# Where the last two tiles of an input projection stand: beside the delta rule's recurrence, or behind it

## The chip, the core and the metric

The kernel runs on one core of a Trainium2 chip. The metric is the device time of one launch in microseconds, the median of several runs, lower is better. The engines are TensorE (PE in the profile; PEld is its weight load), VectorE (DVE), ScalarE (ACT), GpSimd (POOL) and SyncE (SP), which here only issues transfers. Each engine runs its own list of instructions in order.

## The reference, cut to what matters

Two layers of a transformer are applied to 512 latent tokens and 128 context tokens. Four token mixers stand side by side in a layer. They share one input projection `h @ w_in` and one output projection; a SwiGLU follows. The part that matters is the third mixer, a gated delta rule, whose state `s` is carried from one chunk of 64 tokens to the next:

```python
def mix_latent(h, ...):
    (a_q, a_k, a_v, b_q, b_k, b_v, c_qkv, c_g, c_a, c_b, d_cq, d_ckv, d_kr) = project_in(h, p)
    o_a = gqa_attend(...)                 # grouped-query attention
    o_b = natten_latent(b_q, b_k, ...)    # neighbourhood attention
    o_c, _ = deltanet_mixer(c_qkv, ...)   # forward and backward in time
    o_d = block_attention(...)            # latent attention (MLA)
    return concatenate([o_a, o_b, o_c, o_d]) @ p['w_out']

def step(s, xs):                          # the recurrence of deltanet_mixer
    v_new = u_i - einsum('bhcd,bhde->bhce', w_i, s)
    o_i = einsum('bhcd,bhde->bhce', qd_i, s) + einsum('bhij,bhje->bhie', qk_i, v_new)
    s = s * gl_i[..., None, None] + einsum('bhcd,bhce->bhde', kd_i, v_new)
    return s, o_i
```

After the recurrence the result is normalised per head and gated (`rms_norm(o) * silu(z_g)`).

## The kernel before

Activations are kept feature by feature (128 features on the partitions, 640 tokens along the row). Each float32 operand is split into a high and a low part, so a product of a 128-wide tile of the projection with 1024 input features takes 8 blocks x 3 products x 2 halves of the tokens = 48 matmuls; they are the rows `acc<-h,whi` and `acc<-h,wlo`. A tile's weights come by a transfer into `wst` and are split by ScalarE (`whi`) and VectorE (`wlo`).

TensorE's order is written out at build time. Each piece of work is a Python generator that yields what it waits for (an event, a number of free buffers, a moment); `_Order` keeps a clock of its own with estimated costs, and lets the ready generator of the best rank record its next instructions. The order of the other engines is then fixed by the scheduler of the framework. On the chip each engine runs through its list and waits only for data and buffers. So a `yield` in this code is a wait of the recording, not an instruction.

The work around the change, the same in both layers:

- `delta_chain` makes the operands of the delta rule and then calls `scan` over 8 chunks. A step of `scan` is on TensorE `ks`, `qs`, `ysp`, `spp`, `opp`, eight 64x64 matmuls each (16 records in the trace, as float32 is run in two passes), and between them a VectorE sum `xt` (after `ks`), a ScalarE copy `ysb` (after `ysp`) and a VectorE sum `st`, the new state (after `spp`), on which the next `ks` waits.
- `delta_out` then normalises on VectorE (`dno`, `oss`, a reciprocal root of 11 small instructions, `dno`), transposes on TensorE (`otp`) and gates on VectorE (`og`). It is called for chunks 2 to 5 while the last steps of the scan run, and for the rest behind them.
- `rest` records what is left of the input projection: the parts of the grouped-query attention, two gate tiles, one block of the neighbourhood attention's values (`tm_chunk`), and at last four tiles (`wfm` 8 to 11) that go out to memory through `natst` and `dnat` and are read again much later (`nraw`). It has rank 2, so it fills in between the steps of the scan.
- `attention` begins behind the chain: it casts `og` into `oh`, and starts grouped-query attention (`gqa`, two groups of 8 units). A unit is `sc` (4 matmuls; scores), a maximum on VectorE (`sm`), an exponential on ScalarE (`p`), six transposes (`ptp`), copies (`pt`), and for each two units a product with the values (`pvo`, 14). The second group's keys and queries are transposed on TensorE (`gktp`, `gqtp`) and split by ScalarE and VectorE (`gk`, `qst`). When `rest` has ended, buffers are turned over to a second score bank (`psE`) and to the operands of the latent attention (`mkr`, `mcf`, `mcq`, `wkvup`).

Of the kernel before, what the change touches and what calls it, by code (L numbers as in the profile page):

```python
# [288 lines left out]
class _Build:  # L289
# [622 lines left out]
    def delta_chain(self, l, h, S, dn, dt, ps, pd, first):  # L912

        nc, A, od = self.nc, self.A, self.od
        hr = lambda q, k: h[:, q, k]

        qk = S["qk"] = dn.tile([128, 2, 10, 128], F32, name="qk")
        vn = S["vn"] = dn.tile([128, 10, 2, 64], F32, name="vn")
        kt = S["kt"] = dn.tile([128, 10, 2, 64], F32, name="kt")
        S["ss"] = [dt.tile([128, 10, 2], F32, name=f"ss{i}") for i in range(2)]  # L920
        self.M = dn.tile([128, 2, 10, 2, 64], F32, name="dM")
        self.Q = dn.tile([128, 2, 10, 2, 64], F32, name="dQ")

        def features(fts):
            evs = []
            for ft in fts:
                o = yield from self.fm_steps(A["wfm"][l, ft], hr, range(KD), ps)
                evs.append(od.spawn(self.conv_steps(l, ft, o, S, dt, pd), 0))
            return evs

        ev_k = [od.spawn(self.conv_steps(l, ft, o, S, dt, pd), 0) for ft, o in zip((2, 3), first)]

        g0 = dt.tile([128, 5, 16], F32, name="g0")
        lss = S["lss"] = dt.tile([128, 5, 2], F32, name="lss")

        def sink(t, o):
            st = self.cv.tile([128, 648], F32, tag="cv", name="crow", bufs=4)
            nc.scalar.copy(st[:, 0:432], o)
            nc.vector.tensor_copy(g0[:, t], st[:, 416:432])
            nc.sync.dma_start(out=self.dscr["craw"][l, :, t, :], in_=st[:, 0:416])  # L940
            for i, (a, b) in enumerate(((0, 256), (256, 384))):
                j = dt.tile([128, 512], F32, tag="mst", name="msq", bufs=1)
                nc.scalar.activation(j[:, 0:b - a], st[:, a:b], AF.Square, accum_out=lss[:, t, i:i + 1])

        yield od.spawn(self.tm_chunk([A["wtmc"][l, i] for i in range(4)], h, 432, [(ps, "w")] * 5, sink, "cv"), 0, True)
        S["input"].at = od.now
        gz = dt.tile([128, 10, 2, 2, 2], F32, name="gz")
        gv = g0.rearrange("p t (r a) -> p t r a", r=2)
        for r in range(2):
            for cc in range(2):  # L950
                nc.vector.tensor_copy(gz[64 * r:64 * r + 64].rearrange("p (t c) a d q -> p t c (a d q)", c=2)[:, :, cc, :],
                                      gv[64 * cc:64 * cc + 64, :, r, :])
        ev_g = od.spawn(self.gates(l, gz, dn, dt, pd), 0)

        def more(fts, when):
            for e in when:
                yield e
            ev = yield from features(fts)
            for e in ev:
                yield e  # L960

        for e in ev_k + [ev_g]:
            yield e
        self.key_norms(S["ss"][1], dn, dt)
        yield od.via(("ACT", 0.3), ("DVE", 0.4), ("ACT", 0.2))
        evs = [od.spawn(self.chunk_matrices(g, qk, ev_k, dt, pd), 0) for g in range(5)]
        ev_q = od.spawn(more((0, 1), evs[:1]), 0.8, True)
        ev_v = od.spawn(more((4, 5), [S["inv"]]), 0.9, True)
        ev_m = od.spawn(self.query_matrices(qk, evs + [ev_q], pd), 0.7)
        for e in evs:  # L970
            yield e
        S["inv"].at = od.now
        rt = yield from self.inverse16(l, dt)
        yield od.spawn(self.inverse(rt, dt, pd), 0)
        for e in (ev_v, ev_m):
            yield e
        self.query_norms(S["ss"][0], dn, dt)
        nc.vector.tensor_tensor(out=vn, in0=vn, in1=self.nk.unsqueeze(3).to_broadcast([128, 10, 2, 64]), op=ALU.mult)
        S["O"] = dn.tile([128, 10, 2, 64], F32, name="dno")
        s0 = dn.tile([128, 2, 2, 64], F32, tag="st", name="st", bufs=4)  # L980
        nc.sync.dma_start(out=s0, in_=A["st0"][l])

        def prompt():
            sf = yield from self.scan(range(8, 10), None, S, dn, pd)
            nc.sync.dma_start(out=A["ost"][l], in_=sf)
            yield S["gates"]
            yield from self.delta_out(l, [(8, 10)], S, dn, pd)

        def middle():
            yield S["gates"]  # L990
            yield from self.delta_out(l, [(2, 6)], S, dn, pd)

        yield od.via(("DVE", 1.3))
        e = od.spawn(prompt(), 0.5)
        s6 = yield from self.scan(range(6), s0, S, dn, pd)
        em = od.spawn(middle(), 0.5)
        yield from self.scan(range(6, 8), s6, S, dn, pd, range(8))
        yield S["gates"]
        yield from self.delta_out(l, [(0, 2), (6, 8)], S, dn, pd)
        yield e  # L1000
        yield em
# [985 lines left out]
    def mixer(self, l, h, h_st, x, fx, fx_st, P, W, p_side, w_side):  # L1987
# [10 lines left out]
            first = self.start(h, x, fx, ps)  # L1998
        od = self.od = _Order(w=1 if l == 0 else 5, dn=3, ta=3, cv=4, **{t: 0 for t in "sc fd pv wt p pt k0 q0 k1 q1".split()})
        S = {"heads": [], "group": [_Event(), _Event()]}  # L2000
        S.update({k: _Event() for k in ("inv", "gates", "h", "input", "back", "whole")})
        ready = []

        def second_half():
# [27 lines left out]
        def rest():  # L2032
            for c in range(2):
                yield from self.tm_chunk([A["wtma"][l, c, i] for i in range(2)], h, 256, [(ps, "w")] * 3,
                                         lambda t, o, c=c: nc.scalar.copy(ar[:, t, 256 * c:256 * c + 256], o))
            norms.append(od.spawn(self.gqa_norm(l, ar, dn, dt, S["inv"]), -0.5))
            heads.append(od.spawn(ahead(), 0.3))
            for i in range(2):
                o = yield from self.fm_steps(A["wfm"][l, 6 + i], hr, range(KD), ps)
                for hf in range(2):  # L2040
                    nc.scalar.activation(og[:, i, SPLIT[hf]], o[hf], AF.Silu)
                od.give("w", 2, od.via(("ACT", 0.8)))
            S["gates"].at = od.now + 1.0

            def sink_v(t, o):
                st = self.cv.tile([128, 648], F32, tag="cv", name="bvst", bufs=4)
                nc.scalar.copy(st[:, 0:256], o)
                nc.sync.dma_start(out=self.dscr["bv"][l, 128 * t:128 * t + 128], in_=st[:, 0:256])

            yield from self.tm_chunk([A["wtma"][l, 2, i] for i in range(2)], h, 256, [(ps, "w")] * 3, sink_v, "cv")  # L2050
            for i in range(4):
                o = yield from self.fm_steps(A["wfm"][l, 8 + i], hr, range(KD), ps)
                yield "cv", 1
                od.give("cv", at=od.now + 3.0)
                st = self.cv.tile([128, 648], F32, tag="cv", name="natst", bufs=4)
                for hf in range(2):
                    nc.scalar.copy(st[:, SPLIT[hf]], o[hf])
                od.give("w", 2, od.via(("ACT", 0.8)))
                nc.sync.dma_start(out=self.dscr["nat"][l, i], in_=st[:, 0:T])
# [76 lines left out]
        def ahead():  # L2136

            for e in norms[1:]:
                yield e
            S["first"] = yield from self.gqa_operands(l, 0, ar, ma, ma, ps)  # L2140

        chain = od.spawn(self.delta_chain(l, h, S, dn, dt, ps, pd, first), 0)
        norms.append(od.spawn(self.mla_norm(l, dt, ps, S), 1.5))
        ev_r = od.spawn(rest(), 2, True)
        evs = [ev_r] + ([od.spawn(trickle(), 0.4, True)] if l == 0 else [])
        od.spawn(attention(), 0)
# [8 lines left out]
        h = hp.tile([128, 2, KD, T], F32R, tag="h", name="h", bufs=1)  # L2155
# [204 lines left out]
```

## Time and profile before

| | |
|---|---|
| median of 3 runs | 1937.26 us (1935.78 to 1942.27) |
| profiled execution, its own time | 1942.35 us |
| its span | 1940.6 us |
| TensorE busy | 1820.8 us (94%) |
| VectorE, ScalarE, GpSimd busy | 1219.8, 784.7, 512.7 us (63%, 40%, 26%) |
| mean granted TensorE clock | 0.976 |

The profiled execution is one launch; its span is what the profile shows from first to last instruction, and 1.75 us lie around it. Times in the rows below are from the start of the span. Layer 0 lies in the first half, layer 1 in the second; the scan of layer 0 ends near 313 us, that of layer 1 near 1255 us. The granted clock is 1.00 for 2.4 GHz and 0.50 for 1.2 GHz.

### The profile page before, as it was taken

The numbers are of one execution on the slowest core, as the hardware profiler recorded it, in microseconds if no ns is written. First come the engines' busy times: TensorE is split into PE (matmuls) and PEld (weight loads), VectorE is DVE, ScalarE is ACT, GpSimd is POOL, SyncE is SP. The second block draws the span as 40 slices with busy tenths as digits, with TensorE's granted clock in tenths as the row PEclk, the third lists the DMA queues.
The fourth block names the chain that finished last, engine by engine and source line by source line (L and its number), as shares of the span: only waits on it lengthen the run. The fifth ranks groups of instructions, "written<-read, shape, count | busy, mean of one in ns | idle before, by whom it ended". The sixth has DMA issues, their size and how long they took to land.

```text
span 1940.6 us, 40518 instructions
## 1 busy us (share of the span) xinstructions
PE 1820.8 (94%) x16392; PEld 1714.9 (88%) x16392; DVE 1219.8 (63%) x2488; ACT 784.7 (40%) x1627; POOL 512.7 (26%) x648
## 2 busy tenths in 40 slices
PE   5997998899999999999999999879989999999997
PEld 4986787778899999999998988768779999999997
DVE  6573546676557647747745773566757784774874
ACT  4632123676452212212337432267655541442541
POOL 1221431233220000000021363213324451642731
PEclk9997899999999999999999999989999999999999
DMA  8345323133435525625522232213432222222231
GB/s 302 113 123 135 120 91 98 36 95 88 150 109 176 161 84 181 184 77 192 173 100 92 73 92 66 73 37 78 106 129 89 66 88 76 88 80 82 78 97 55
DMA packets 114171, 210.38 MB, mean 108 GB/s; under 512 B 44160, under 2 KB 61312, under 8 KB 113856
## 3 DMA queue, kind: packets, MB, share of 16 engines
q1 hardware_dynamic: 105920, 202.74, 33.3%
q0 software_dynamic: 2816, 4.72, 1.2%
q8 instruction: 129, 2.11, 0.4%
q10 hardware_dynamic: 5248, 0.33, 0.2%
q14 instruction: 58, 0.48, 0.1%
HBM read 183.14 MB, written 19.89 MB: 105 GB/s over the span
## 4 chain that ended last, share of the span: by engine, by line
PE 77%; DVE 9%; ACT 5%; DMA 5%; issue 2%; SPq 0%; POOL 0%; DVEq 0%; ACTq 0%; POOLq 0%
PE acc L366 55%; PE tacc L366 6%; PE pvo L366 3%; PE ptp L378 3%; PE sc L366 2%; DMA wst<-wout 1%; PE mpart L366 1%; PE invp L366 1%; DVE wlo L310 1%; ACT p L1421 1%; ACT whi L309 1%; DMA wmd<-wmod 1%; DMA wmd<-wmodT 1%; ACT pt L1456 1%; PE ysp L366 1%
## 5 line engine op out<-in xcount | busy, mean ns | idle before, releaser
L366 PE MATMUL acc<-h,whi 128*128 128x256 f32 (+1 forms) x2304 | 453.9, 315 | 3.3 <-ACT h L589 1.4
L366 PEld LDWEIGHTS acc<-h,whi 128*128 128x128 f32 x2304 | 381.1, 191 | 11.9 <-issue 3.4
L309 ACT CAST whi<-wst 128x1024 fp32r<-128x1024 f32 (+3 forms) x164 | 156.9, 958 | 446.1 <-PE acc L366 398.1
L366 PE MATMUL acc<-h,wlo 128*128 128x256 f32 (+1 forms) x1152 | 274.1, 313 | 3.4 <-DVE wlo L310 3.4
L310 DVE TENSOR_TENSOR wlo<-wst,whi 128x1024 fp32r<-128x1024 f32 (+3 forms) x164 | 190.5, 1163 | 99.5 <-ACT whi L309 98.9
L366 PE MATMUL acc<-g,whi 128*128 128x256 f32 (+1 forms) x1128 | 216.7, 309 | 0.3 <-DVE g L310 0.3
L366 PEld LDWEIGHTS acc<-h,wlo 128*128 128x128 f32 x1152 | 211.3, 190 | 5.0 <-DVE wlo L310 3.9
L1937 DVE SCALAR_TENSOR_TENSOR x<-acc,mods,x 128x256 f32<-128x256 f32 (+1 forms) x192 | 75.3, 434 | 196.9 <-PE acc L366 196.8
L556 POOL TENSOR_TENSOR sq<-sq 128x256 f32<-128x256 f32 (+1 forms) x48 | 45.7, 952 | 541.4 <-ACT sq L550 541.1
L366 PEld LDWEIGHTS acc<-g,whi 128*128 128x128 f32 x1128 | 185.9, 188 | 0.5 <-DVE g L310 0.5
L522 DVE SCALAR_TENSOR_TENSOR wmj<-wmd,cb 128x1024 f32<-128x1024 f32 x112 | 136.8, 1222 | 37.2 <-DMA wmd<-wmodT 35.9
L366 PE MATMUL tacc<-whi,h 128*128 128x256 f32 (+1 forms) x640 | 151.0, 317 | 0.3 <-ACT whi L309 0.3
L366 PE MATMUL acc<-h,sw 128*128 128x320 f32 x912 | 143.6, 309 | 0.0
L366 PEld LDWEIGHTS acc<-h,sw 128*128 128x128 f32 x912 | 136.6, 188 | 0.0
L366 PE MATMUL acc<-g,wlo 128*128 128x384 f32 (+1 forms) x564 | 135.2, 309 | 0.0
L366 PEld LDWEIGHTS tacc<-whi,h 128*128 128x128 f32 x640 | 111.2, 194 | 11.1 <-issue 6.4
L366 PE MATMUL acc<-oh,whi 128*128 128x384 f32 (+1 forms) x512 | 115.7, 316 | 5.3 <-ACT whi L309 3.4
L1424 POOL TENSOR_SCALAR dg<-cbase,sd 128x128 f32<-128x128 f32 x96 | 58.7, 612 | 209.3 <-DVE sd L1422 144.7
L366 PE MATMUL acc<-tt,sw 128*128 128x320 f32 x684 | 109.5, 309 | 0.0
L378 PE MATMUL ptp<-cbase,p 128*128 128x128 f32 x512 | 81.6, 286 | 28.2 <-ACT pt L1456 14.4
L366 PEld LDWEIGHTS acc<-g,wlo 128*128 128x128 f32 x564 | 103.3, 188 | 0.0
L366 PEld LDWEIGHTS acc<-tt,sw 128*128 128x128 f32 x684 | 102.6, 188 | 0.0
(361 smaller groups left out, 3426.4 us busy)
## 6 DMA issues: line engine op xcount, KB each, us to landing
wmd<-wmodT SPq DMA_DIRECT2D x56, 512.0 KB
wst<-wg SPq DMA_DIRECT2D x44, 512.0 KB
wst<-wu SPq DMA_DIRECT2D x44, 512.0 KB
wmd<-wmod SPq DMA_DIRECT2D x40, 512.0 KB
wst<-wd SPq DMA_DIRECT2D x34, 448.0 KB
wst<-wfm SPq DMA_DIRECT2D x24, 512.0 KB
wst<-wd SPq DMA_DIRECT2D x16, 512.0 KB
wst<-wtma SPq DMA_DIRECT2D x12, 512.0 KB
```

What stands on the lines that cost most here:

```text
L309: self.nc.scalar.copy(hi, src)
L310: self.nc.vector.tensor_tensor(out=lo, in0=src, in1=hi.bitcast(F32), op=ALU.subtract)
L366: self.nc.tensor.matmul(out, lhsT, rhs, start=start, stop=stop)
L378: self.nc.tensor.transpose(out, in_, self.ident)
L522: nc.vector.scalar_tensor_tensor(out=j, in0=st, scalar=1.0, in1=self.cb[:, g], op0=ALU.mult, op1=ALU.mult, accum_out=self.msum[:, e, g:g + 1])
L556: (eng or nc.gpsimd).tensor_tensor(out=self.sq[hf][0], in0=self.sq[hf][0], in1=sq, op=ALU.add)
L1421: nc.scalar.activation(p, s, AF.Exp, bias=m, accum_out=d)
L1424: nc.gpsimd.tensor_scalar(out=dg, in0=self.ident, scalar1=d, scalar2=None, op0=ALU.mult)
L1456: nc.scalar.copy(pt[:, a:a + m].rearrange("p a b -> p (a b)"), tp[:, :128 * m])
L1937: self.nc.vector.scalar_tensor_tensor(out=x_out[:, a:b], in0=o[h][:, a - HB * h:b - HB * h], scalar=m[:, 8 * gate + e, grp:grp + 1], in1=x ...
```

## The change

`delta_chain` sets a new event, `S["scan"]`, when the last step of the scan has been recorded, and `rest` waits for it ahead of the third of its last four tiles. So the last two tiles (96 matmuls `acc<-h`, their casts and copies) are recorded behind the scan in both layers.

```diff
@@ delta_chain
         yield from self.scan(range(6, 8), s6, S, dn, pd, range(8))
+        S["scan"].at = od.now
         yield S["gates"]
         yield from self.delta_out(l, [(0, 2), (6, 8)], S, dn, pd)
@@ mixer
-        S.update({k: _Event() for k in ("inv", "gates", "h", "input", "back", "whole")})
+        S.update({k: _Event() for k in ("inv", "gates", "h", "input", "back", "whole", "scan")})
@@ rest
             for i in range(4):
+                if i == 2:
+
+                    yield S["scan"]
                 o = yield from self.fm_steps(A["wfm"][l, 8 + i], hr, range(KD), ps)
```

No instruction, transfer or semaphore is added; rows change their place. Lines of the changed kernel stand one to four lower (L1348 becomes L1349). TensorE, layer 1, the end of the scan and what follows it, before:

```order
L366 MATMUL acc<-h,wlo 128x256
L366 MATMUL acc<-h,wlo 128x384
L366 MATMUL ks<-st,qk 64x64 x8
L366 MATMUL qs<-st,qk 64x64 x8
L366 MATMUL otp<-cbase,dno 64x64 x8
L366 MATMUL ysp<-xt,dM 64x64 x8
L366 MATMUL otp<-cbase,dno 64x64 x8
L366 MATMUL spp<-ysb,kd 64x64 x8
L366 MATMUL opp<-ysb,dQ 64x64 x8
L366 MATMUL otp<-cbase,dno 64x64 x16
L366 MATMUL sc<-gk,qst 128x512 x2
L366 MATMUL sc<-gk,qst 128x256 x2
```

The same place now:

```order
L366 MATMUL spp<-ysb,kd 64x64 x8
L366 MATMUL opp<-ysb,dQ 64x64 x8
L366 MATMUL ks<-st,qk 64x64 x8
L366 MATMUL qs<-st,qk 64x64 x8
L366 MATMUL otp<-cbase,dno 64x64 x8
L366 MATMUL ysp<-xt,dM 64x64 x8
L366 MATMUL otp<-cbase,dno 64x64 x8
L366 MATMUL spp<-ysb,kd 64x64 x8
L366 MATMUL opp<-ysb,dQ 64x64 x8
L366 MATMUL acc<-h,whi 128x256
L366 MATMUL acc<-h,whi 128x384
```

From the middle of the scan's fifth step on, no `acc<-h` stands between its rows in layer 1; the 96 that stood there follow as 80 ahead of the last `otp` x16, 10 behind it, then the first `sc` (4), the last 6 and the second `sc`. In layer 0, where 66 stood behind the scan before, it is 78, `otp` x16, 10 (6 before), `sc`, 8, `sc`, and 24 are gone from the last step and a half.

ScalarE, layer 1, from the cast of the gated result (`oh<-og`) to the first exponential, before:

```order
L362 CAST oh_14630<-og 128x640
L309 CAST gk<-gck 128x256
L362 CAST oh_14630<-og 128x640
L1421 ACT_TABLE_LOAD
L1421 ACTIVATE p,sd<-sc,sm 128x768
```

And now (`whi<-wst` 128x512 are casts of weights for the latent attention and the output projection, `natst<-acc` copies the last tile out):

```order
L362 CAST oh_14620<-og 128x640
L309 CAST gk<-gck 128x256
L362 CAST oh_14620<-og 128x640
L309 CAST whi<-wst 128x512
L2061 COPY natst<-acc 128x256
L2061 COPY natst<-acc 128x384
L309 CAST whi<-wst 128x512
L1422 ACT_TABLE_LOAD
L1422 ACTIVATE p,sd<-sc,sm 128x768
```

Two casts and the copies of the last tile have moved in ahead of the first exponential; layer 0 had them there already.

TensorE, layer 1, where the second group's keys and queries are turned over, before:

```order
L378 MATMUL ptp<-cbase,p 128x128 x4
L378 MATMUL gktp<-cbase,ar 128x128 x4
L378 MATMUL ptp<-cbase,p 128x128 x2
L366 MATMUL sc<-gk,qst 128x512 x2
L366 MATMUL sc<-gk,qst 128x256 x2
L378 MATMUL gqtp<-cbase,ar 128x128 x4
L366 MATMUL pvo<-pt,gcv 64x128 x4
```

And now:

```order
L378 MATMUL ptp<-cbase,p 128x128 x12
L366 MATMUL pvo<-pt,gcv 64x128 x4
L366 MATMUL pvo<-pt,ar 64x128 x8
L366 MATMUL pvo<-dg,ones 64x128 x2
L378 MATMUL gktp<-cbase,ar 128x128 x4
L378 MATMUL gqtp<-cbase,ar 128x128 x4
L366 MATMUL acc<-mcq,whi 128x256
```

`gktp` and `gqtp` stood among the first group's units; now they stand behind all eight of them, six `acc<-mcq` follow, and then `sc` of the second group. It is the same in layer 0. From the first `sc<-mk,mq` of the latent attention on, the order is the one of before in both layers.

## Rows read from the trace of the kernel before

**Rows 1.** The page: shares of the chain that ended last, by engine.

```profile
PE 77%; DVE 9%; ACT 5%; DMA 5%; issue 2%; SPq 0%; POOL 0%; DVEq 0%; ACTq 0%; POOLq 0%
```

**Rows 2.** Stretches: start and end, length, busy PE to POOL, clock, DMA.

```profile
345.00:366.00 21.00, 17.57 (x160) 14.79 (x159) 12.96 (x26) 14.32 (x36) 3.55 (x6) 0.92 0.03 6
...
1255.20:1266.80 11.60, 2.47 (x34) 1.97 (x32) 6.35 (x24) 1.37 (x3) 0.86 (x2) 0.68 0.22 73
...
1282.00:1304.00 22.00, 19.21 (x171) 16.26 (x171) 14.19 (x28) 15.12 (x38) 3.83 (x7) 0.92 0.03 5
```

**Rows 3.** TensorE by time, layer 1: start, length, work [idle before <-releaser].

```profile
1228.28 0.68 PE L366 MATMUL ysp<-xt,dM 64*64 64x64 f32 x16
...
1250.79 0.68 PE L366 MATMUL ks<-st,qk 64*64 64x64 f32 x16
...
1252.87 0.68 PE L366 MATMUL ysp<-xt,dM 64*64 64x64 f32 x16 [0.47 <-DVE xt L1331]
...
1254.09 0.68 PE L366 MATMUL spp<-ysb,kd 64*64 64x64 f32 x16
1254.60 0.63 PE L366 MATMUL opp<-ysb,dQ 64*64 64x64 f32 x16
1263.47 0.69 PE L366 MATMUL otp<-cbase,dno 64*64 64x64 f32 x8 [8.24 <-DVE dno L1396]
...
1266.80 2.90 PE L366 MATMUL sc<-gk,qst 128*128 128x512 f32 x8
...
1329.38 1.30 PE L366 MATMUL sc<-mk,mq 96*128 96x512 f32 x6
```

**Rows 4.** TensorE by time, layer 0, from the scan's end.

```profile
313.08 0.85 PE L366 MATMUL acc<-h,whi 128*128 128x256 f32 x4
...
322.89 0.45 PE L366 MATMUL otp<-cbase,dno 64*64 64x64 f32 x8
...
326.31 0.87 PE L366 MATMUL sc<-gk,qst 128*128 128x512 f32 x4
331.19 1.65 PE L366 MATMUL sc<-gk,qst 128*128 128x512 f32 x4 [4.01 <-ACT p L1421]
...
392.20 1.30 PE L366 MATMUL sc<-mk,mq 96*128 96x512 f32 x6
```

**Rows 5.** ScalarE by time, layer 0 and layer 1.

```profile
327.06 0.61 ACT L309 CAST whi<-wst 128x512 fp32r<-128x512 f32 x1
...
330.15 0.90 ACT L1421 ACTIVATE p<-sc,sm 128x768 f32<-128x768 f32 x1
...
1250.61 0.62 ACT L309 CAST whi<-wst 128x512 fp32r<-128x512 f32 x1 [6.57 <-PE acc L366]
...
1270.21 0.90 ACT L1421 ACTIVATE p<-sc,sm 128x768 f32<-128x768 f32 x1
...
1283.16 0.58 ACT L1593 CAST gk<-gktp 64x512 fp32r<-64x512 f32 x1
```

**Rows 6.** VectorE by time, layer 0 and layer 1.

```profile
307.19 0.85 DVE L1331 SCALAR_TENSOR_TENSOR xt<-ks,neg,vn 128x64 f32<-128x64 f32 x4
...
1241.94 0.68 DVE L1389 TENSOR_TENSOR dno<-dno,rq 128x512 f32<-128x512 f32 x1
...
1247.98 0.91 DVE L1396 TENSOR_TENSOR dno<-dno,ors 128x512 f32<-128x512 f32 x1
...
1254.89 0.42 DVE L1358 TENSOR_TENSOR st<-spp,st 128x256 f32<-128x256 f32 x1 [0.35 <-PE spp L366]
...
1284.38 0.69 DVE L1540 TENSOR_TENSOR gk<-gktp,gk 64x512 fp32r<-64x512 f32 x1
```

**Rows 7.** TensorE's clock: two stretches, and a row ahead of the first.

```profile
1175.05 1.91 PE L366 MATMUL invp<-rt,ivy 32*32 32x32 f32 x64
...
1177.60:1184.00 6.40, 6.40 (x56) 6.05 (x56) 2.16 (x4) 3.07 (x9) 0.00 (x0) 0.50 0.01 3
...
1240.00:1255.20 15.20, 14.66 (x244) 13.36 (x242) 10.53 (x33) 4.87 (x10) 3.18 (x6) 1.00 0.32 97
```

## The prediction

> **What bounds the kernel now.** I read the page first: the chain that ended last runs through TensorE for 77% of the span [rows 1], so what a change does to TensorE's waits is what it does to the time. Then I read TensorE in order of time around the end of the scan in each layer, because there the two layers differ. In layer 1 the projection runs out with the scan: the last `acc<-h` ends ahead of `ks` at 1250.79, the scan ends at 1254.60 + 0.63 = 1255.23, and then TensorE waits 8.24 us for VectorE's normalisation [rows 3]. In that stretch of 11.60 us it is busy for 2.47 us, and its granted clock averages 0.68, that is, it fell from 2.4 to 1.2 GHz [rows 2]. In layer 0 the same normalisation is hidden: 66 `acc<-h` run from 313.08 to 322.89, and `otp` follows without a wait [rows 4]. This also gives the price of such a matmul in a dense run: 9.81 / 66 = 0.149 us. The reader is to see that layer 1 has a hole of 8 us which the moved tiles fit, and that layer 0 has none.
>
> **Taking the tiles out of the scan, layer 1.** A step without filler is a loop of waits. The last step of before is nearly one: `ks` to `ysp` 2.08 us, `ysp` to `spp` 1.22 us [rows 3], `spp` to the end of `st` 1254.89 + 0.42 - 1254.09 = 1.22 us [rows 3, 6], with about 0.1 us to the next `ks`, 1.3 us; 4.6 us in all. Without filler stand the tail of one step, two whole steps and the last step, which lasts 4.44 us as before (1250.79 to 1255.23): 1.22 + 1.3 + 2 x 4.6 + 4.44 = 16.2 us. VectorE has the normalisation of the middle chunks in between: `dno` of 0.68 us, a reduction about as long, eleven small instructions 0.2 us apart and `dno` of 0.91 us (first and last in [rows 6]), some 4.5 us that the state's sums can stand behind. The trace of before doesn't show how much of it lands on the path; nothing is the lower bound, 4.5 the upper, and I take 2.5, as several of the instructions fit while TensorE works. Two `acc<-h` fewer let the stretch begin at 1228.28 - 0.30 = 1228.0, so the scan ends at 1228.0 + 18.7 = 1246.7, 8.5 us earlier. 94 matmuls of 0.149 us, 14.0 us, were taken out; the other 5.5 us are new idle time in the scan.
>
> **Behind the scan, layer 1.** 80 matmuls take 11.9 us, to 1258.6. They cover the normalisation, which needs 8.24 us (to 1254.9); without this cover it would cost those 8.24 us again. `otp` to `sc` takes 2.5 us at full clock (layer 0: 326.31 - 322.89 = 3.42, less its 6 `acc<-h` of 0.9), then 10 `acc<-h` 1.5 us: the first `sc` starts at 1262.6, where it was 1266.80 [rows 3]. The hole pays 4.2 us up to here.
>
> What is late next is the first exponential. Behind `oh` on ScalarE now stand a weight cast, the copies of the last tile, another cast, and only then `p`. Such a cast waits for the buffer of the last tile: in before it started at 1250.61, released by `acc` [rows 5]. The last `acc<-h` ends at 1262.6 + 0.87 + 0.9 = 1264.4. Layer 0 had this order already: from the cast at 327.06 to the end of `p` at 331.05 it took 3.99 us [rows 5]. So `p` ends at 1268.5, where it ended at 1271.11: 2.6 us are left of the gain. Behind `p` waits the second `sc`, because the second score bank comes only when `rest` has ended; layer 0 shows this as a wait of 4.01 us [rows 4]. From the end of `p` to the first `sc<-mk` layer 0 took 392.20 - 331.05 = 61.15 us, layer 1 took 1329.38 - 1271.11 = 58.27 us [rows 3 to 5]. With layer 0's order I take layer 0's pace: +2.9 us. Layer 1 comes out at -2.6 + 2.9 = +0.3 us.
>
> **Layer 0.** 24 `acc<-h` leave the last step and a half. `xt` of the last step (307.19, to 308.04) I take as unchanged; `ysp` follows at 308.25, `spp` 1.22 us later, and 1.14 us after that the scan ends [rows 3, 6]: 310.6, not 313.08. 78 x 0.149 = 11.6 us bring `otp` to 322.2 (322.89 before); 10 `acc<-h` where 6 stood bring the first `sc` to 326.2, and the 8 behind it end at 326.2 + 0.87 + 1.2 = 328.3. The weight cast that started at 327.06 [rows 5] now waits for them, so `p` and the second `sc` are 1.4 us later: **+1.4 us**.
>
> **The turn to the second group, both layers.** `gktp` and `gqtp` now stand behind all units of the first group, so the second group can't overlap it. What is left open on TensorE: about 0.8 us for the last copy ahead of `pvo` (a `pt` copy is as long as the `gk` cast, 0.58 us, and waits 0.2 us), and behind `gktp` the split of keys and queries: a cast of 0.58 us, four differences of 0.69 us [rows 5, 6] and a cast of the result between them, 3.9 us, covered by `gqtp` (0.6) and six `acc<-mcq` (0.9), so 2.4 us. Together 3.2 us a layer. Against it, waits inside the first group may go, since the splitting no longer stands between its units: TensorE idled 21.00 - 17.57 = 3.4 us in layer 0's stretch and 22.00 - 19.21 = 2.8 us in layer 1's [rows 2]. If none goes the cost is 3.2 us, if all go it is nothing; I take half, 1.5 us a layer, **+3.0 us**.
>
> **At nothing:** the weights of the moved tiles are transferred and split while the tiles ahead of them run, as before. `natst` and `dnat` come some 14 us later and are read only in the neighbourhood attention, far behind. The loads of the latent attention (`mkr`, `mcf`) start with the end of `rest`, some 4 us ahead of their first cast; if they aren't there, `p` isn't held up, as they stand behind it, but the next units are.
>
> **Sum.** 0.3 + 1.4 + 3.0 = +4.7 us on the profiled execution's 1942.35 us (span 1940.6 and 1.75 around it): 1947.1 us. This execution stands 5.1 us above the median of the runs, so for the median: 1937.26 + 4.7 = **1942.0 us**. The idle time is given back in three places. Bounds of the open terms: the scan from -2.5 to +2.0 us, layer 1's pace from -2.9 us to nothing, the turns from -3.0 to +3.4 us. Not all will fall one way; half of the sums gives the forecast's own range, 1938 to 1945 us.
>
> **Rivals.** *B, the clock falls in the bare scan.* Small matmuls don't always hold it: after a stretch mostly of 32x32 matmuls, TensorE busy, it stood at 0.50 for 6.40 us [rows 7]. Against it, the mean clock up to the end of the last, bare step of layer 1's scan was still 1.00 [rows 7]. Now 19 us are bare. A stretch as in the row costs half of its busy 6.40 us, 3.2 us; one that takes three steps (`ks`, `ysp` and `spp` each 0.5 us longer, 1.5 a step) and a part of the dense run costs 6. In the middle, +4.5 on the forecast: 1946.5 us.
>
> The Trainium skill says on the page "TensorE: Matmul & The Clock Gate", section "Why this matters for your kernels", that matmul bursts should not be parted by idle gaps, or the engine drops to its half clock. By this rule the bare scan, where TensorE waits for two other engines in each step, is what to avoid, and the time would be B's; by the row up to 1255.2 us the clock holds. No row of this case shows four bare steps in turn, so it keeps a chance of its own.
>
> *C, faster.* The first group's units, freed of the splitting, run without those waits, the turn costs nothing, and layer 1 keeps its own pace: -2.6 - 2.8 - 3.4 + 1.4 = -7.4 us, 1929.9 us. For it speaks the 8.24 us hole, the largest wait in this part; against it that ScalarE's list holds the first exponential back. It decides if the second group's first `sc` comes no later than before in relation to the first group's last `pvo`.
>
> *D, the hole only moves.* The turns cost nothing net and the rest stands: 0.3 + 1.4 = +1.7 us, 1939.0 us.
>
> **How the numbers follow.** A launch varies by some tenths of a per cent here, so a difference under 0.3%, 5.8 us, can't be told from none (1931.5 to 1943.1). Forecast 0.35: no change 0.24, slower 0.11. B 0.27: slower 0.23, no change 0.04. C 0.18: faster 0.16, no change 0.02. D 0.20: no change 0.17, faster 0.03. Together faster 0.19, no change 0.47, slower 0.34. The range leaves out the outer part of C and of B, about 0.1 each: 1929 to 1951 us.
>
> **What would show it.** In the profile of the changed kernel: no wait of 8 us for `dno` in layer 1; idle time of about 5.5 us between `ks`, `ysp` and `spp` from 1228 us on; the scan's end 8.5 us earlier; the second `sc` of layer 1 waiting for `p` for some 4 us; waits behind `gktp` in both layers; the first `sc<-mk` of layer 0 about 3 us and that of layer 1 about 5 us later than before. A granted clock under 0.8 in the scan is B. A first `sc<-mk` of layer 1 that comes earlier than 1329.38 means that the forecast is wrong: then the turn, or the pace behind `p`, was priced too high.

## The result, and the profile after

The changed kernel takes 1954.79 us (median of 8 runs, 1947.75 to 1958.60), the kernel before 1938.91 us in the same series. The ratio is 1.0091 (95% interval 1.0072 to 1.0111): slower, by 15.9 us between the two medians and by 17.6 us if the ratio is taken. That is outside the forecast's range, which ended at 1951 us. The profiled execution has a span of 1956.5 us, 15.9 us more than before.

The chain that ended last, from the page of the changed kernel (shares of the span), beside [rows 1]:

```profile
PE 78%; DVE 9%; ACT 5%; DMA 4%; issue 2%; POOL 1%; SPq 1%; DVEq 0%; ACTq 0%; POOLq 0%
```

It is still TensorE's chain, so the loss has to be found on TensorE in order of time. TensorE of the changed kernel in layer 1, from the bare steps of the scan to the second group's turn (start, length, work, idle before and its releaser), beside [rows 3]:

```profile
1236.55 0.68 PE L366 MATMUL ysp<-xt,dM 64*64 64x64 f32 x16
1238.39 0.68 PE L366 MATMUL spp<-ysb,kd 64*64 64x64 f32 x16 [1.16 <-ACT ysb L1349]
...
1239.67 0.68 PE L366 MATMUL ks<-st,qk 64*64 64x64 f32 x16
...
1242.19 0.68 PE L366 MATMUL spp<-ysb,kd 64*64 64x64 f32 x16 [0.55 <-ACT ysb L1349]
...
1243.45 0.68 PE L366 MATMUL ks<-st,qk 64*64 64x64 f32 x16
...
1246.97 0.68 PE L366 MATMUL spp<-ysb,kd 64*64 64x64 f32 x16 [1.54 <-ACT ysb L1349]
...
1249.10 1.12 PE L366 MATMUL ks<-st,qk 64*64 64x64 f32 x16 [0.97 <-DVE st L1359]
...
1254.61 0.92 PE L366 MATMUL opp<-ysb,dQ 64*64 64x64 f32 x16
...
1267.32 0.45 PE L366 MATMUL otp<-cbase,dno 64*64 64x64 f32 x8
...
1271.32 0.87 PE L366 MATMUL sc<-gk,qst 128*128 128x512 f32 x4
...
1276.96 1.65 PE L366 MATMUL sc<-gk,qst 128*128 128x512 f32 x4 [3.89 <-ACT p L1422]
...
1282.56 1.65 PE L366 MATMUL sc<-gk,qst 128*128 128x512 f32 x4 [2.67 <-ACT p L1422]
...
1286.70 0.97 PE L366 MATMUL sc<-gk,qst 128*128 128x512 f32 x4 [1.22 <-ACT p L1422]
...
1292.98 0.97 PE L366 MATMUL sc<-gk,qst 128*128 128x512 f32 x4 [1.48 <-ACT p L1422]
...
1299.29 0.97 PE L366 MATMUL sc<-gk,qst 128*128 128x512 f32 x4 [1.50 <-ACT p L1422]
...
1305.58 0.66 PE L378 MATMUL gktp<-cbase,ar 128*128 128x128 f32 x4
...
1309.67 1.07 PE L366 MATMUL acc<-mcq,whi 128*128 128x384 f32 x3 [2.87 <-DVE gk L1541]
...
1311.07 2.55 PE L366 MATMUL sc<-gk,qst 128*128 128x512 f32 x8
```

Up to the first `sc` things went nearly as forecast. Behind it, each `sc` starts when the exponential `p` of the unit ahead is over; two units' scores next to each other (`x8`) come only at 1311.07, for the second group. In [rows 3] the first `sc` was such an x8. The exponentials show it (ScalarE of the changed kernel, layer 1):

```profile
1275.92 0.90 ACT L1422 ACTIVATE p<-sc,sm 128x768 f32<-128x768 f32 x1
...
1281.52 0.89 ACT L1422 ACTIVATE p<-sc,sm 128x768 f32<-128x768 f32 x1
...
1285.65 0.91 ACT L1422 ACTIVATE p<-sc,sm 128x768 f32<-128x768 f32 x1
...
1288.76 0.90 ACT L1422 ACTIVATE p<-sc,sm 128x768 f32<-128x768 f32 x1 [0.73 <-DVE sm L1419]
...
1291.94 0.90 ACT L1422 ACTIVATE p<-sc,sm 128x768 f32<-128x768 f32 x1
```

1281.52 + 0.89 = 1282.41, and `sc` starts at 1282.56; 1285.65 + 0.91 = 1286.56, and `sc` starts at 1286.70; 1291.94 + 0.90 = 1292.84, and `sc` starts at 1292.98. That is one score bank (a bank here is the buffer for the scores of one unit), with `sc`, maximum and exponential in turn: 3.1 to 3.2 us from one `sc` to the next once it runs freely.

That pace alone is not the loss. These are the eighth and the ninth exponential of layer 1 on ScalarE, before:

```profile
1294.58 0.90 ACT L1421 ACTIVATE p<-sc,sm 128x768 f32<-128x768 f32 x1 [0.79 <-DVE sd L1422]
...
1297.76 0.90 ACT L1421 ACTIVATE p<-sc,sm 128x768 f32<-128x768 f32 x1
```

and in the changed kernel:

```profile
1301.37 0.90 ACT L1422 ACTIVATE p<-sc,sm 128x768 f32<-128x768 f32 x1 [2.13 <-DVE sm L1419]
...
1313.64 0.90 ACT L1422 ACTIVATE p<-sc,sm 128x768 f32<-128x768 f32 x1 [4.62 <-DVE sm L1419]
```

From the first exponential to the eighth it takes 25.45 us now and took 24.37 us before (from 1275.92 and, in [rows 5], 1270.21); in layer 0 it is 25.52 and was 26.96. So the eight units themselves are hardly slower on one bank. What is late is what now stands behind them: from the eighth exponential to the ninth it takes 12.27 us where it took 3.18 (layer 0: 12.40 and 5.78), and from there to the first `sc<-mk` of the latent attention 32.70 us where it took 31.62 (34.34 and 29.31).

The waits of TensorE over the whole execution, changed kernel (total us, times, longest):

```profile
PE sc L366 <- ACT p L1422: 22.7, 10, 3.9
PE ptp L378 <- ACT p L1422: 7.0, 10, 1.3
PE acc L366 <- DVE gk L1541: 5.8, 2, 2.9
```

Before, `sc` waited for `p` once, 4.01 us [rows 4]. Now it does so ten times, five a layer.

Counted from the first `ks` of a layer, so that what a launch does earlier falls out:

| us | layer 0 before | after | layer 1 before | after |
|---|---|---|---|---|
| first `ks` to the scan's end | 67.60 | 64.33 | 65.60 | 57.33 |
| to the first `sc` | 80.77 | 79.84 | 77.17 | 73.12 |
| first `sc` to first `sc<-mk` | 65.89 | 77.14 | 62.58 | 75.02 |
| first `ks` to the last `sc<-nk` | 249.91 | 260.69 | 244.56 | 251.95 |

So 0.9 and 4.1 us are won up to the first `sc`, and 11.3 and 12.4 us are lost between it and the first `sc` of the latent attention. That last stretch in layers 0 and 1, before (start and end, length, busy PE to POOL, clock, DMA):

```profile
326.31:392.20 65.89, 53.45 (x446) 45.85 (x445) 42.97 (x84) 47.34 (x106) 15.79 (x27) 0.92 0.26 72
1266.80:1329.38 62.58, 51.90 (x446) 44.33 (x445) 40.60 (x82) 45.87 (x102) 15.15 (x27) 0.95 0.20 51
```

and in the changed kernel:

```profile
322.99:400.13 77.14, 57.64 (x460) 49.29 (x459) 43.73 (x86) 47.53 (x106) 16.37 (x28) 0.89 0.22 61
1271.32:1346.34 75.02, 55.88 (x458) 47.34 (x457) 43.63 (x86) 47.11 (x106) 15.73 (x28) 0.91 0.22 63
```

TensorE is idle there for 7.1 and 8.5 us more than before, and busy for 4.2 and 4.0 us more. Of the busy time the 8 and 6 moved `acc<-h` that fall into it are 1.2 and 0.9 us; the rest comes with the lower mean clock, at which the same four `sc` took 1.65 us (1282.56) and not 0.97 (1286.70).

### The profile page after: what moved, and what is told of

It reads as the page before. It is cut to its first block, busy times and chain, and to the rows that moved or that the text cites. A ratio compares the mean times of both kernels' runs of the same rounds, so it can differ in the third digit from the quotient of the medians.

```text
span 1956.5 us, 40518 instructions
## 1 busy us (share of the span) xinstructions
PE 1825.0 (93%) x16392; PEld 1720.2 (88%) x16392; DVE 1223.5 (63%) x2488; ACT 783.6 (40%) x1627; POOL 514.1 (26%) x648
## 3 DMA queue, kind: packets, MB, share of 16 engines
q0 software_dynamic: 2816, 4.72, 1.2%
## 4 chain that ended last, share of the span: by engine, by line
PE 78%; DVE 9%; ACT 5%; DMA 4%; issue 2%; POOL 1%; SPq 1%; DVEq 0%; ACTq 0%; POOLq 0%
PE acc L366 54%; PE tacc L366 7%; PE pvo L366 3%; PE sc L366 3%; PE ptp L378 3%; ACT p L1422 1%; PE invp L366 1%; PE mpart L366 1%; DVE wlo L310 1%; DMA wst<-wout 1%; DVE sm L1419 1%; ACT whi L309 1%; PE ysp L366 1%; PE spp L366 1%; DVE nt L586 1%
## 5 line engine op out<-in xcount | busy, mean ns | idle before, releaser
L1422 ACT ACTIVATE p<-sc,sm 128x768 f32<-128x768 f32 (+1 forms) x96 | 79.7, 830 | 50.8 <-DVE sm L1419 45.4
```

The source lines that it names most:

```text
L1422: nc.scalar.activation(p, s, AF.Exp, bias=m, accum_out=d)
```

## The experiments

Medians of different series differ by some us (the kernel before had 1938.9, 1940.6, 1941.0 and 1938.7 us), so kernels are compared by their ratios to it. Three theories of that loss. *Bank*: the second score bank, and all that `attention` opens with it, comes only when the first group's eight units are over. In the code, `attention` has rank 0 but is not marked dense, and the planner, when its own estimate of TensorE's activity is low, takes a ready dense generator ahead of it:

```python
                elif best is None:
                    best = t
                    if t[5] or self.heat * math.exp((self.beat - self.now) / 3.4) > 3700:
                        break
                elif t[5]:          # t[5]: dense
                    best = t
                    break
```

The units are dense. Before, `rest` was over when the units began (layer 1) or with the first of them (layer 0), and `attention` opened the bank at once. *ScalarE*: casts of the latent attention's operands wait for their loads and hold the exponentials. *Scan*: the bare scan, with the clock, is the loss.

**1. `attention` dense, tiles moved as in the change.**

```diff
-        od.spawn(attention(), 0)
+        od.spawn(attention(), 0, True)
```

> The changed kernel, with attention given the planner's priority for dense work, so that the second score bank opens ahead of the second unit, as in layer 0 of before (on the kernel before the same edit alters no row of TensorE's order). Bank theory (the loss comes from eight units that go through one score bank, 3.1 us a unit or more, and from all that is recorded behind them): from the first sc to the first sc<-mk about 65.9 us in both layers (77.1 and 75.0 in the changed kernel), so 11 and 9 us come back, and the time is that of before within 4 us: 1935 to 1941. ScalarE theory (casts of the latent attention's operands wait for their loads and hold the exponentials): the waits of the third and fourth sc for p, 5.1 and 3.9 us, stay, and 7 us at most come back: 1946 to 1950. Scan theory (the bare scan and its clock are the loss): no change from the changed kernel, 1953 to 1957.

Measured: 1938.20 us, ratio 0.9997 (0.9975 to 1.0019). First `sc` to first `sc<-mk` is 65.61 and 65.82 us. The waits of the whole execution:

```profile
PE sc L366 <- ACT p L1422: 7.8, 2, 3.9
```

Two waits are left of ten, one a layer. One word to the planner gives back the whole loss, with the tiles behind the scan and the scan as bare as before (57.28 us in layer 1). Scan and ScalarE fall as main causes.

**2. The kernel before, with the bank and all that `attention` opens with it late.** The second group's turn is not late here.

```diff
+            yield self.first_group      # set when the first group's eight units are over
             for e in evs:
                 yield e
             yield "w", 5
```

> The kernel before, no tile moved; only attention waits for the first group's units before it opens the second score bank. Bank theory: the first group's units follow each other no faster than one in 3.1 us, and the first sc to the first sc<-mk takes 4 to 12 us longer a layer, as the second group's turn still lies inside the first group here: 1946 to 1962. ScalarE theory: the loads are not behind a late acc here, so little is lost: 1937 to 1943. Scan theory: nothing, 1937 to 1941.

Measured: 1960.42 us, ratio 1.0094 (1.0063 to 1.0125): as large a loss as the change's, with no tile moved and the turn in its old place. First `sc` to first `sc<-mk` is 70.68 and 71.24 us. Here the wait is seen one step later, at the transposes of `p`:

```profile
PE ptp L378 <- ACT p L1421: 32.8, 22, 5.1
```

**3. The changed kernel, latent attention's copies and splits on GpSimd.**

```diff
-        nc.scalar.copy(kp[64:96], ...)
+        nc.gpsimd.tensor_copy(kp[64:96], ...)
-            self.split(krs ...), self.split(cq ...), self.split(ckv ...)
+            self.split_pool(krs ...), self.split_pool(cq ...), self.split_pool(ckv ...)
```

> The changed kernel, with the copies and splits of the latent attention's operands (mkp, mkrs, mcq, mckv) on GpSimd, so that no exponential stands behind a load on ScalarE or a sum on VectorE. ScalarE theory: the third and fourth sc no longer wait beyond the pace of one bank (3.1 us from sc to sc): 2 to 4 us a layer come back, 1947 to 1951. Bank theory: the sc still follow each other at 3.1 us or more and the turn stays: at most 3 us come back in all, 1951 to 1956. Scan theory: no change, 1953 to 1957.

Measured: 1957.94 us, ratio 1.0095 (1.0064 to 1.0127): nothing comes back. The first `pvo` comes 0.9 us earlier after the first `sc` than in the changed kernel in both layers (15.64 for 16.63, 15.43 for 16.28), and it is lost again behind it. The casts held the exponentials for a moment, but they don't set the time.

**4. One tile behind the scan instead of two** (`if i == 3:`). `rest` then ends ahead of the first unit.

> Only the last tile waits for the end of the scan. Layer 0's order stays that of before; in layer 1 48 acc<-h stand behind the scan, rest ends ahead of the first unit, and sc comes eight at a time as before. Bank theory: with the second bank in time the filled hole (8.24 us, of which 48 acc<-h cover 7.1) is a gain: two steps of the scan go bare, first sc of layer 1 3 to 6 us earlier, same pace behind it: 1933 to 1937. Scan theory: half of the changed kernel's loss in layer 1, 1941 to 1946. ScalarE theory: as the bank theory.

Measured: 1937.13 us, ratio 0.9991 (0.9971 to 1.0012). Layer 1 reaches its first `sc` 73.58 us after the first `ks` (77.17 before): 3.6 us earlier, as the bank theory wants; the whole kernel's gain is too small to tell from none. TensorE in layer 1 shows what takes part of it away:

```profile
1240.91 0.63 PE L366 MATMUL qs<-st,qk 64*64 64x64 f32 x16
1245.14 1.12 PE L366 MATMUL otp<-cbase,dno 64*64 64x64 f32 x16 [3.60 <-DVE dno L1397]
```

In TensorE's list an `otp` of the middle chunks stands ahead of the last step's `ysp`, and VectorE isn't done with it.

**5 to 7. What the late `attention` carries.** Three things come late with it: the second bank, the operands of the latent attention, whose products fill in between the units, and (with the planner's low estimate) the second group's turn. The fifth kernel is the first experiment with the bank alone withheld, the sixth with the operands alone withheld, the seventh is the changed kernel with the turn early:

```diff
 5: one bank until the first group is over
-            ps.pools.update(w=..., sc=[(pc, "sc"), (pe, "sc")], fd=...)
+            ps.pools.update(w=..., fd=...)      # sc of pe is given when first_group is set
 6: operands late
     def mla_operands(...):
+        yield self.first_group
 7: changed kernel, turn early
-            ev_g = od.spawn(self.gqa(...), 1)
+            ev_g = od.spawn(self.gqa(...), 1, True)
```

> The repaired kernel of the first experiment (attention with the priority for dense work), but the second score bank is withheld until the first group's eight units are over; everything else that attention opens comes on time, so the second group's keys and queries and the latent attention's first products fill in. If the one bank is what costs: the eight units still start 3.1 us or more apart, first sc to first sc<-mk 70 to 77 us a layer, and 8 to 20 us come back on top of the repaired kernel's 1938: 1946 to 1958. If the bank is harmless as long as there is other work to fill in: within 4 us of the repaired kernel, 1934 to 1942.

> The repaired kernel with the second score bank on time, but the operands of the latent attention (mkr, mcf, mcq, wkvup and the products acc<-mcq) are recorded only when the first group's eight units are over, as in the changed kernel. If the late operands are what costs: first sc to first sc<-mk 70 to 77 us a layer, 1946 to 1958. If it is the bank: within 4 us of the repaired kernel's 1938, 1934 to 1942.

> The changed kernel; the second group's turn (gktp, gqtp) gets the priority for dense work and so stands behind the first pair of units again; the second bank stays late. If the turn is what costs (the forecast took 1.5 us a layer for it): the waits of 2.9 us behind gktp go and 3 to 8 us come back, 1946 to 1952. If it is the bank: the units stay 3.1 us or more apart and less than 4 us come back, 1951 to 1956.

| | us | ratio to before (95%) | first `sc` to `sc<-mk`, layers 0, 1 |
|---|---|---|---|
| 1, all on time | 1938.20 | 0.9997 (0.9975 to 1.0019) | 65.61, 65.82 |
| 5, bank late | 1949.27 | 1.0039 (1.0020 to 1.0059) | 69.46, 68.99 |
| 6, operands late | 1947.14 | 1.0042 (1.0021 to 1.0062) | 70.29, 69.36 |
| 7, turn early, rest late | 1953.69 | 1.0060 (1.0037 to 1.0083) | 73.36, 73.59 |
| changed kernel, all late | 1954.79 | 1.0091 (1.0072 to 1.0111) | 77.14, 75.02 |

The times of the fifth and the sixth both lie in the range that I had given if theirs was the cause (1946 to 1958), at its low end. Against the first experiment, the late bank costs 3.9 and 3.2 us a layer, the late operands 4.7 and 3.5; from the changed kernel to the seventh the turn gives back 3.8 and 1.4. Together 20.5 us, where the changed kernel stands 11.5 + 9.2 = 20.7 above the first. By the ratios the seventh kernel gets back a third of the loss, more than the 4 us that I allowed for if the turn were harmless, but its interval and the changed kernel's overlap. So by these stretches the loss is shared: about a third the bank, four tenths the operands, a quarter the turn. That the parts add up isn't shown: each was taken with other things late beside it, and the second experiment loses as much as the change without the turn. In the sixth, the late operands are felt at the turn, which has nothing left to cover it:

```profile
PE ptp L378 <- DVE gk L1541: 7.1, 2, 3.9
```

My bank theory was right on what is late, and too narrow on why it costs: with other work to fill in, one bank alone doesn't lose half of it. Such a stretch varies between launches: in three kernels with layer 0's order of before it took 65.89, 64.70 (fourth) and 67.73 us (eleventh), so a share is good to some 1.5 us, and the turn's 1.4 us in layer 1 is no more than that.

**8 to 10. A better place for the normalisation.** In the kernel of the first experiment, `middle` (the normalisation of chunks 2 to 5) waits for the end of the scan too, with two tiles moved, none, and one:

```diff
         def middle():
+            yield S["scan"]
             yield S["gates"]
```

> The repaired kernel, with the normalisation of the middle chunks (delta_out for chunks 2 to 5) behind the scan as well, under the 96 acc<-h. In the changed kernel the steps of layer 1's bare scan took 3.79, 5.65 and 6.4 us; if VectorE's normalisation and the half clock that followed made the difference, all take about 3.8 us, the scan of layer 1 ends 4 us earlier than in the repaired kernel, and the time is 1930 to 1935. If the bare steps are long by themselves, or the normalisation only comes out behind the 96 matmuls, no change: 1936 to 1940.

> The eighth experiment without the moved tiles: the normalisation of the middle chunks behind the scan, all four tiles where the kernel before has them as far as the planner lets them (in layer 1 only 6 acc<-h stand behind the scan). If the eighth's gain comes from the two tiles that cover the normalisation: here layer 1 waits 8 us or more for dno with nothing to cover it, 1939 to 1946. If it comes from moving the normalisation alone: 1930 to 1936.

> The eighth experiment with one tile behind the scan instead of two. 48 acc<-h, 7.1 us, cover the normalisation of eight chunks, which takes 8 us for four chunks and some 3 us more for the others: layer 1 waits 2 to 5 us for dno, but one of the scan's bare steps is covered again: 1933 to 1938, no better than two tiles.

| | us | ratio to before (95%) | layer 1, first `ks` to scan's end, to first `sc` |
|---|---|---|---|
| 8, two tiles | 1935.13 | 0.9974 (0.9953 to 0.9994) | 54.52, 72.43 |
| 9, none | 1936.60 | 0.9991 (0.9970 to 1.0011) | 63.50, 78.36 |
| 10, one tile | 1933.52 | 0.9963 (0.9941 to 0.9985) | 58.51, 69.01 |

The tenth is faster than the kernel before, by about 7 us (3 to 11 by its interval). It doesn't wait 2 to 5 us for `dno`, as I had expected; its end of the scan, TensorE in layer 1, and the two stretches from the bare part to the first `sc` (start and end, length, busy PE to POOL, clock, DMA):

```profile
1241.53 0.63 PE L366 MATMUL opp<-ysb,dQ 64*64 64x64 f32 x16
1242.54 0.68 PE L366 MATMUL ks<-st,qk 64*64 64x64 f32 x16 [0.37 <-DVE st L1360]
...
1245.06 0.68 PE L366 MATMUL spp<-ysb,kd 64*64 64x64 f32 x16 [0.55 <-ACT ysb L1350]
1245.58 0.63 PE L366 MATMUL opp<-ysb,dQ 64*64 64x64 f32 x16
...
1253.34 0.45 PE L366 MATMUL otp<-cbase,dno 64*64 64x64 f32 x8
...
1256.71 1.66 PE L366 MATMUL sc<-gk,qst 128*128 128x512 f32 x8
```

```profile
1238.49:1246.21 7.72, 6.25 (x162) 5.66 (x161) 5.20 (x16) 2.80 (x6) 2.30 (x6) 1.00 0.27 87
1246.21:1256.71 10.50, 9.57 (x113) 9.04 (x112) 9.15 (x40) 2.54 (x6) 0.88 (x2) 1.00 0.16 36
```

In the eighth the bare steps took 3.79, 4.72 and 4.54 us, not 3.8 each, and the scan ended 2.8 us earlier than in the first experiment, not 4. Its time falls between the two ranges that I had given. The second of these steps and the clock of the last show why (the wait on TensorE, what ScalarE did ahead of `ysb`, and the last two steps as stretches):

```profile
1233.69 0.68 PE L366 MATMUL spp<-ysb,kd 64*64 64x64 f32 x16 [1.55 <-ACT ysb L1350]
```

```profile
1232.66 0.63 ACT L1392 ACTIVATE vn<-dno 128x512 f32<-128x512 f32 x1 [3.81 <-DVE dno L1391]
```

```profile
1230.17:1234.89 4.72, 3.12 (x81) 2.82 (x81) 2.74 (x10) 0.89 (x2) 1.73 (x4) 1.00 0.00 0
1234.89:1239.43 4.54, 4.00 (x81) 3.74 (x81) 2.10 (x8) 0.37 (x1) 1.45 (x3) 0.62 0.01 4
```

The normalisation is recorded behind the scan, but the framework still places its first `dno` and `vn` inside it, and `ysb` stands behind `vn` on ScalarE. In the tenth, with the reduction and the root behind the scan, two bare steps take 7.7 us at full clock, the 48 `acc<-h` cover VectorE's work (9.15 us busy in 10.50), and the first `sc` x8 takes 1.66 us. In [rows 3] it took 2.90 us, in the half clock behind the 8.24 us hole. Without a moved tile (ninth) the wait for `dno` is 8.7 us, and layer 1 gains nothing up to the first `sc`. Its time is still below the 1939 to 1946 us that I had expected, as layer 1 takes only 59.98 us from there to the first `sc<-mk`; why that stretch is 2.6 us shorter than before I haven't settled. Eighth and tenth can't be told apart by their intervals, and the first differs from the eighth by less than these resolve.

**11. The change in layer 1 alone** (`if i == 2 and l == 1:`).

> The change in layer 1 alone; the order of layer 0 is that of before. If the layers' shares are those that the two profiles show (10.8 us and 7.4 us from the first ks to the last sc), 5 to 10 us slower than before: 1943 to 1949. If layer 1 gains by its filled hole, as the forecast's third rival had it, and layer 0 loses all: 1930 to 1937.

Measured: 1951.96 us, ratio 1.0065 (1.0043 to 1.0087), above the 5 to 10 us expected. Layer 1 takes 77.73 us from the first `sc` to the first `sc<-mk`, against 75.02 in the changed kernel. Layer 1 with its filled hole loses as well, so rival C, the one that lived on this hole, is out. Layer 0 is longer too, 253.05 us from the first `ks` to the last `sc<-nk` where it took 249.91 with the same order; I haven't found out why.

## Why the prediction was wrong, step by step

- **The scan without filler** (right in sum by luck, wrong in parts). From the first bare row to the end I had 18.7 us; it took 1254.61 + 0.92 - 1236.55 = 18.98. A step is 3.78 us where nothing stands in the way (1239.67 to 1243.45), not 4.6; the next two took 5.65 and 6.4. The bare parts alone come to 3.12 + 2 x 3.78 + 4.44 = 15.1 us, where I had 16.2. The normalisation adds 1.9, where I had 2.5 for VectorE alone: about half is the sum `st` behind VectorE's small instructions (`ks` waits 0.97 us), and the other half is ScalarE, where `ysb` stands behind the `vn` below (`spp` waits 1.54 us, not 0.55). The half clock adds 2.0 us in the last step, for which the sum had nothing.

  ```profile
  1245.94 0.63 ACT L1391 ACTIVATE vn<-dno 128x512 f32<-128x512 f32 x1 [3.80 <-DVE dno L1390]
  ```

  Measured from the first `ks`, the scan ends 8.27 us earlier (8.5 forecast).
- **Up to the first exponential** (right in layer 1, a little too dear in layer 0; 1264.4 + 3.99 is 1268.4 and not the forecast's 1268.5, which changes nothing). The first `sc` of layer 1 comes 4.05 us earlier (4.2 forecast), `p` ends 2.9 us earlier (2.6). In layer 0 `p` ends 0.1 us later where I had 1.4. The wait of the second `sc` for `p` in layer 1 is 3.89 us (some 4).
- **"With layer 0's order I take layer 0's pace"** is the step that failed. I took the missing second bank for a wait of one unit, because I held that it opens when `rest` has ended. It opens when the planner lets `attention` run, and with the units ready first that is behind all eight. All else that `attention` opens then comes late too, behind units that are hardly slower. From the end of the first `p` to the first `sc<-mk` I had 61.15 + 1.5 = 62.65 us in both layers; it took 400.13 - 328.77 = 71.36 us in layer 0 and 1346.34 - 1276.82 = 69.52 in layer 1. That is 15.6 us more, all of the error and a little over: the parts up to there came out 1.6 us better than forecast.
  By the Trainium skill's page "Perfetto Trace Analysis", section "Matmuls", independent groups of matmuls should rotate through different PSUM banks, so that reading one out overlaps the next group's matmuls. The trace agrees: on one bank `sc` waits ten times for the exponential that reads it, 22.7 us, and withholding the second bank alone costs 3.9 and 3.2 us a layer.
- **The turn to the second group** (mis-sized, and a symptom). I priced it alone, at 1.5 us of at most 3.2 a layer, and set against it that the first group would run more freely. The 2.87 us behind `gktp` are the split that I bounded. But from the eighth exponential to the ninth are 12.27 us in layer 1, 9.1 more than before, and 12.40 in layer 0, 6.6 more: the first group runs out for 4.2 us ahead of `gktp` (1305.58), the turn lasts 5.5 us to the next `sc` (1311.07), and 2.6 us later its exponential starts. By the seventh experiment the early turn alone gets back only 3.8 and 1.4 us of the stretch; where the rest goes then I haven't followed. Nor did the first group make up for it by running more freely: to its eighth exponential it took 1.4 us less in layer 0 and 1.1 us more in layer 1. I saw that `gktp` had moved behind eight units and didn't ask what else had to be late for that.
- **"At nothing"**: the loads of the latent attention were in time for `p`, and the case that I named, that the next units are held, did occur for a moment (third experiment, 0.9 us a layer, given back behind).
- **Rival B, the clock**: it did fall. The stretches of the bare steps, changed kernel, layer 1:

```profile
1236.55:1240.33 3.78, 2.49 (x71) 2.22 (x72) 2.11 (x4) 1.78 (x4) 1.10 (x3) 1.00 0.35 120
1240.33:1243.45 3.12, 2.46 (x66) 2.12 (x60) 1.66 (x7) 0.37 (x1) 1.47 (x5) 1.00 0.17 49
1243.45:1249.10 5.65, 3.13 (x81) 2.83 (x81) 4.57 (x18) 0.89 (x2) 1.73 (x4) 0.94 0.00 0
1249.10:1255.50 6.40, 6.30 (x113) 6.08 (x113) 4.31 (x15) 0.37 (x1) 1.87 (x3) 0.52 0.01 3
```

  TensorE was busy for 0.66 and 0.79 of the first two stretches at 1.00; after the third, busy for 0.55, it ran the last step at 1.2 GHz, which took 6.4 us instead of the 4.44 of before. So about 2 us in the scan, not 4.5. The Trainium skill's page "TensorE: Matmul & The Clock Gate", section "Why this matters for your kernels", warns of idle gaps between matmul bursts. The trace agrees that the clock drops here, but it held through the first two of these stretches. The first experiment keeps this loss and still has the time of before: B, the clock of the bare scan, is not what made the kernel slow.
- **The signs listed**: the wait of 8 us for `dno` is gone, idle time of 18.95 - 14.38 = 4.6 us stands in the bare steps (5.5), the second `sc` waits, `gktp` is followed by a wait, and the clock is under 0.8 in the last step, B's sign. The first `sc<-mk`, counted from the first `ks` of its layer, came 10.3 and 8.4 us late. The forecast's 3 and 5 us were counted through both layers, so by layer it had 2.9 and 1.8: that is where it could be told wrong.
- The two profiles' spans differ by 15.9 us: 10.8 in layer 0, 7.4 in layer 1, less 2.4 ahead of the first `ks`, where the two programs have the same order on TensorE.

## What to carry to other kernels

When a planner fixes the order, a moved piece of work also moves what the planner opens after it: ask of every wait at build time what is recorded behind it (here a score bank, a set of operands, a second group), and read in the new order whether it still comes when the old one had it. A stretch in which one instruction repeats singly where it stood in pairs is such a sign, and the question is then what used to run beside it and now stands behind it: here the eight units took as long as before, and the loss came after them. Filler moved out of a recurrence paid here, by 0.3 to 0.4%, only where the normalisation that it covers was moved behind the recurrence as well (eighth and tenth experiment); without that, one tile (fourth) or two (first) couldn't be told from none.

## What the runs showed of the hardware that I had not expected

In the changed kernel the clock didn't fall in the first two bare stretches of the scan (1.00, with TensorE busy for 0.66 and 0.79 of the time), fell in the third (0.94), and averaged 0.52 through a last step in which TensorE was busy for 6.30 of 6.40 us. In the eighth it fell later and less: 1.00 in the step of 4.72 us, 0.62 in the last. In the tenth kernel two bare steps in 7.72 us ran at 1.00 throughout. And launches differ early: the first `ks` of layer 0 starts between 240.4 and 249.0 us in the profiled executions of the kernels here, though TensorE's order is the same up to it in all of them, so stages are better compared from such a row than from the start of the span.
